# Chunks of 2048 columns in two PSUM buffers, two by two, and the first two stores as one, in an add-and-GELU kernel

## The chip, the cores and the metric

The kernel runs on one core of a Trainium2 chip. The rounds of runs were taken on several chips, each time together with the kernel before, so runs of different rounds are compared by their ratios to it. The metric is the device time in microseconds (us), median over several executions. All runs quoted are fast, with a granted clock of 1.00. The "span" of a profile is one execution as the hardware profiler saw it; it is 1.8 us below the device time of the same execution for the kernel before (120.5 for 122.32); spans compare only to within 0.3 us. A transfer "lands" when the profile has it complete.

Three compute queues and one transfer queue matter here. DVE is the vector engine, ACT the scalar (activation) engine and POOL is GpSimd; SP is the sync engine, which here only issues the transfers. The 16 transfer engines are called DMA in the profile.

## The reference

```python
x, y: float32 [1024, 4096]
z = x + y
out = 0.5 * z * (1 + tanh(sqrt(2/pi) * (z + 0.044715 * z**3)))
```

This is 33.55 MB of reads and 16.78 MB of writes for very little arithmetic. The kernel computes the same function as z * sigmoid(z * (c1 + c1 * 0.044715 * z^2)), with c1 = 2 * sqrt(2/pi).

## The kernel before

The inputs are viewed as 128 partitions of 32768 columns. x is loaded into one large buffer z, and the result is written over it. y goes through two buffers of 8192 columns in turn. The columns are worked on in chunks, each with five steps on three engines; `wt` holds the intermediate value of a chunk in PSUM.

```python
YS = 8192
CH = 1024
PS = 4                                    # PSUM buffers of one chunk
loads = [2048, 6144, 8192, 8192, 8192]    # columns, for x and for y
stores = [8192, 8192, 8192, 4096, 4096]
by_pool = set(range(1, C))                # chunk 0 is added by DVE, all others by POOL
# ... cut ...
def add(c):  # POOL:  z = z + y
def sq(c):   # ACT:   w = (root * z)^2        into PSUM
def stt(c):  # DVE:   w = (w + c1) * z
def sig(c):  # ACT:   w = sigmoid(w)
def mul(c):  # DVE:   z = w * z
# ... cut ...
for i in range(-3, C + 1):
    if 0 <= i < C:
        dve.append((stt, i))
        acts.append((sig, i))
    if 0 <= i - 1 < C:
        dve.append((mul, i - 1))
    # ... cut: the add of chunk 0 ...
    if 0 <= i + 2 < C:
        acts.append((sq, i + 2))

needs = {
    load_y: ...  # the adds that still read this y buffer
    add: ...     # the loads of these columns
    sq: lambda c: [(add, c)] + ([(mul, c - PS)] if c >= PS else []),
    store: lambda i: [(mul, c) for c in over(cr, *sr[i])],
    # ... cut ...
}
```

Every engine works through its own list strictly in order, so these lists are the schedule. In words, DVE alternates: stt of chunk i, then multiply of chunk i-1. The square of a chunk must wait until the PSUM buffer is free, that is, until the multiply of the chunk PS earlier has read it. The SP queue holds all loads, then all stores.

## Time and profile before

| | before |
|---|---|
| time, median (first 3 runs) | 122.37 us (122.04 to 122.44) |
| span of the profiled run | 120.5 us |
| DVE, ACT, POOL busy | 63%, 53%, 61% |
| transfer engines busy | 98.1% |
| moved | 50.33 MB, 418 GB/s over the span |
| last y load lands | 80.9 us |
| last store issued, landed | 104.19, 120.0 us |

Compute is over at 104 us, and the last store lands nearly 16 us later. The prediction below goes through the lines.

### The profile page before, as it was taken

The page shows a single profiled execution, that of the slowest core. Times are in us where ns is not written, and L with a number is a line of the kernel's source. Part 1 is how long each engine was busy: PE and PEld are TensorE (multiplying, and loading weights), DVE is VectorE, ACT ScalarE, POOL GpSimd, SP SyncE. Part 2 cuts the span into 40 slices and gives each one's busy share as a digit, 9 for nine tenths or more (in the row PEclk, how much of TensorE's full clock was granted, in tenths as well). Part 3 has the DMA queues.
Part 4 walks back from the last instruction along what each step waited for, and adds up shares of the span by engine and source line. Part 5 has one row for each costly group of instructions (what it writes and reads, how often), then busy time and mean ns, then how long its engine had stood idle before and what let it go on. Part 6 is the DMA issues. An engine that isn't in the chain of part 4 may idle for free.

```text
span 120.5 us, 247 instructions
## 1 busy us (share of the span) xinstructions
DVE 75.5 (63%) x66; ACT 63.8 (53%) x66; POOL 73.0 (61%) x35
## 2 busy tenths in 40 slices
DVE  0044700059999009999996999995999999500000
ACT  4016200078875048788758888883878888100000
POOL 0056000699990299999979999949999990000000
DMA  6999999989898989898989899999999999998994
GB/s 201 430 457 449 440 416 446 468 381 489 348 522 348 522 348 522 348 511 359 500 370 489 381 478 391 359 402 459 394 468 402 468 402 468 391 478 364 430 435 174
DMA packets 2162, 50.35 MB, mean 418 GB/s; under 512 B 240, under 2 KB 240, under 8 KB 240
## 3 DMA queue, kind: packets, MB, share of 16 engines
q1 hardware_dynamic: 2160, 50.33, 98.1%
q14 instruction: 2, 0.02, 0.0%
HBM read 33.55 MB, written 16.78 MB: 418 GB/s over the span
## 4 chain that ended last, share of the span: by engine, by line
DMA 49%; POOL 17%; DVE 16%; SPq 1%; ACT 1%; issue 0%; POOLq 0%
DMA y<-in_y_dram 49%; POOL z L131 17%; DVE z L151 8%; DVE w L142 8%; ACT w L136 1%; SPq L114 1%; SPq L121 0%; POOLq L131 0%
## 5 line engine op out<-in xcount | busy, mean ns | idle before, releaser
L131 POOL TENSOR_TENSOR z<-z,y 128x1024 f32<-128x1024 f32 x31 | 72.8, 2387 | 26.3 <-DMA y<-in_y_dram 26.3
L142 DVE SCALAR_TENSOR_TENSOR w<-w,z 128x1024 f32<-128x1024 f32 x32 | 39.4, 1232 | 21.3 <-ACT w L136 21.3
L136 ACT ACTIVATE w<-z 128x1024 f32<-128x1024 f32 x32 | 32.9, 1028 | 37.5 <-POOL z L131 31.6
L151 DVE TENSOR_TENSOR z<-w,z 128x1024 f32<-128x1024 f32 x32 | 38.8, 1215 | 0.0
L147 ACT ACTIVATE w<-w 128x1024 f32<-128x1024 f32 x32 | 31.4, 981 | 0.4 <-DVE w L142 0.4
L131 DVE TENSOR_TENSOR z<-z,y 128x1024 f32<-128x1024 f32 x1 | 1.2, 1226 | 6.0 <-DMA y<-in_y_dram 6.0
L190 ACT ACT_TABLE_LOAD x1 | 1.3, 1283 | 1.3 <-PEq L222 1.3
L189 DVE MEMSET one<- 128x1 f32 x1 | 0.1, 59 | 1.3 <-PEq L222 1.3
L222 POOL MEMSET const-float32-0.0<- 128x1 f32 x1 | 0.1, 98 | 0.2 <-issue 0.2
L190 ACT ACTIVATE one<-one 128x1 f32<-128x1 f32 x1 | 0.2, 203 | 0.0
L222 POOL MEMSET const-bfloat16-1.0<- 128x1 bf16 x1 | 0.1, 101 | 0.0
L222 POOL MEMSET const-uint8-127<- 128x1 uint8 x1 | 0.1, 101 | 0.0
L222 POOL MEMSET const-float32-1.0<- 128x1 f32 x1 | 0.1, 98 | 0.0
## 6 DMA issues: line engine op xcount, KB each, us to landing
z<-in_x_dram SPq DMA_DIRECT2D x3, 4096.0 KB, 34.1
y<-in_y_dram SPq DMA_DIRECT2D x3, 4096.0 KB, 24.8
out_dram<-z SPq DMA_DIRECT2D x3, 4096.0 KB, 30.6
out_dram<-z SPq DMA_DIRECT2D x2, 2048.0 KB, 17.5
z<-in_x_dram SPq DMA_DIRECT2D x1, 3072.0 KB, 13.4
y<-in_y_dram SPq DMA_DIRECT2D x1, 3072.0 KB, 20.3
z<-in_x_dram SPq DMA_DIRECT2D x1, 1024.0 KB, 4.9
y<-in_y_dram SPq DMA_DIRECT2D x1, 1024.0 KB, 6.9
```

Of the source, the lines that this page charges most:

```text
L114: nc.sync.dma_start(out=zt[:, a:b], in_=xv[:, a:b])
L131: eng.tensor_add(out=zt[:, a:b], in0=zt[:, a:b], in1=yt[s][:, o : o + b - a])
L136: nc.scalar.activation(out=wt[c], in_=zt[:, a:b], func=act.Square, scale=root)
L142: nc.vector.scalar_tensor_tensor(out=wt[c], in0=wt[c], scalar=c1, in1=zt[:, a:b], op0=alu.add, op1=alu.mult)
L147: nc.scalar.activation(out=wt[c], in_=wt[c], func=act.Sigmoid)
L151: nc.vector.tensor_mul(out=zt[:, a:b], in0=wt[c], in1=zt[:, a:b])
L189: nc.vector.memset(one, 0.0)
L190: nc.scalar.activation(out=one, in_=one, func=act.Sigmoid)
L222: nc = _bacc.Bacc("TRN2", target_bir_lowering=False, num_devices=1)
```

## The change

The intent is fewer, longer instructions: chunks of 2048 columns halve the number of instructions on three engines, so the fixed cost of each is paid half as often. Two buffers of 8 KB per partition take the same room in PSUM as the four of 4 KB before. The engines' order becomes two by two. The first two stores become one of 8 MiB, with rows of 64 KB.

```diff
-    CH = 1024
-    PS = 4
+    CH = 2048
+    PS = 2
     loads = [2048, 6144, 8192, 8192, 8192]
-    stores = [8192, 8192, 8192, 4096, 4096]
+    stores = [16384, 8192, 4096, 4096]
...
-    dve, acts = [], []
-    for i in range(-3, C + 1):
-        ... (the loop above)
+    dve = [(add, c) for c in range(C) if c not in by_pool]
+    acts = [(sq, 0), (sq, 1)]
+    for c in range(0, C, 2):
+        dve += [(stt, c), (stt, c + 1), (mul, c), (mul, c + 1)]
+        acts += [(sig, c), (sig, c + 1)]
+        if c + 2 < C:
+            acts += [(sq, c + 2), (sq, c + 3)]
```

More of the change, by code (lines that the diff above doesn't have):

```diff
@@ L158 @@
     pool = [(add, c) for c in range(C) if c in by_pool]
-    dve, acts = [], []
-    for i in range(-3, C + 1):
-        if 0 <= i < C:
-            dve.append((stt, i))
-            acts.append((sig, i))
-        if 0 <= i - 1 < C:
-            dve.append((mul, i - 1))
-        if 0 <= i + 3 < C and i + 3 not in by_pool:
-            dve.append((add, i + 3))
-        if 0 <= i + 2 < C:
-            acts.append((sq, i + 2))
+    dve = [(add, c) for c in range(C) if c not in by_pool]
[5 more added lines that the diff above has]
+            acts += [(sq, c + 2), (sq, c + 3)]
     needs = {
```

## The prediction

> **What bounds the kernel now.** I read the page first for shares, then the issues of transfers, then the time stretched over windows, then the chain of waits.
>
> The page has three compute engines at 53 to 63% of the span, and the transfer engines at 98%:
>
> ```profile
> DVE 75.5 (63%) x66; ACT 63.8 (53%) x66; POOL 73.0 (61%) x35
> ...
> DMA  6999999989898989898989899999999999998994
> ...
> q1 hardware_dynamic: 2160, 50.33, 98.1%
> HBM read 33.55 MB, written 16.78 MB: 418 GB/s over the span
> ```
>
> The row of tenths shows no slice below 8 between the first and the last two: the one queue, which carries all loads and then all stores, never runs dry. To see whether it is also at full speed I cut the span at the moments where the stores land. Columns: stretch in us, its length, busy time and count of DVE, ACT and POOL, clock, DMA share, GB/s.
>
> ```profile
> 4.00:80.90 76.90, 53.78 (x47) 45.21 (x47) 54.30 (x23) 1.00 1.01 430
> 80.90:91.10 10.20, 8.63 (x8) 7.12 (x8) 10.08 (x5) 1.00 1.01 435
> 91.10:100.70 9.60, 9.60 (x10) 8.13 (x10) 8.44 (x4) 1.00 0.99 427
> 100.70:110.40 9.70, 3.46 (x3) 1.82 (x2) 0.00 (x0) 1.00 0.98 424
> 110.40:115.30 4.90, 0.00 (x0) 0.00 (x0) 0.00 (x0) 1.00 1.01 431
> ```
>
> It holds 424 to 435 GB/s from 4 us on, and the last column does not care that compute stops at 104 us. So the bound is transfers. The ends add little: about 2 us before data flows, 1.6 us from the last bytes to the end of the span.
>
> The chain of waits could mislead. It says y loads 49%, then POOL adds, then DVE, and its last pieces are:
>
> ```profile
> 100.68 1.18 DVE w L142
> 101.86 2.30 DVE z L151 x2
> ```
>
> It stops at 104.2 us, where the last store is issued; that store lands 15.8 us later. A 2 MiB store needs 4.8 us at 435 GB/s, so most of the 15.8 us is standing in the queue behind earlier stores. That is the slack. I asked for each store's issue and its time to landing:
>
> - store 1, 4 MiB: issued 60.46, 30.6 us to landing, lands 91.1
> - store 2, 4 MiB: 66.75 + 33.9 = 100.7
> - store 3, 4 MiB: 86.84 + 23.5 = 110.3
> - store 4, 2 MiB: 96.08 + 19.1 = 115.2
> - store 5, 2 MiB: 104.19 + 15.8 = 120.0
>
> They land 9.6, 9.6, 4.9 and 4.8 us apart: 4.19 MB / 9.6 us = 437 GB/s, whatever the time of issue. The last load lands at 60.03 + 20.85 = 80.9 us and store 1 lands 10.2 us after it, so loads and stores are one unbroken train.
>
> **What the Trainium skill says.** "DMA: Bandwidth & Descriptors", section "Where 436 GB/s comes from", puts the ceiling of 16 ports at 435.2 GB/s. The trace agrees: 435 in the stretch of store 1, and 437 by landings. 50.33 MB at that ceiling are 115.7 us, of a span of 120.5.
>
> "VectorE: DVE Perf Modes", section "The TRN2 errata", gives an fp32 two-tensor operation (N+151)/0.96 ns, 2291 measured at N=2048. At N=1024 this is 1224; the trace has 1215 and 1232, so I use 2.29 us for one of 2048. Successive ones overlap: the trace's spacing is about 1.14 us for 1.22, so I use 2.21 us for the spacing.
>
> "ScalarE: Activation LUTs", section "What ACT_TABLE_LOAD costs", gives 0.833 ns per element beside a fixed part. The trace at 1024 has 1028 (square) and 981 (sigmoid); 1024 more elements add 853 ns, so 1.88 and 1.83 us.
>
> "SBUF — State Buffer", section "Who interferes with whom", says that a DVE instruction with two SBUF inputs contends with a POOL one that reads SBUF. The trace agrees: the first POOL add, beside the DVE's add at 7.4 us, took 3.39 us against a mean of 2.39.
>
> **The change, part by part.** The rows that it concerns:
>
> ```profile
> L131 POOL TENSOR_TENSOR z<-z,y 128x1024 f32<-128x1024 f32 x31 | 72.8, 2387 | 26.3 <-DMA y<-in_y_dram 26.3
> L142 DVE SCALAR_TENSOR_TENSOR w<-w,z 128x1024 f32<-128x1024 f32 x32 | 39.4, 1232 | 21.3 <-ACT w L136 21.3
> L136 ACT ACTIVATE w<-z 128x1024 f32<-128x1024 f32 x32 | 32.9, 1028 | 37.5 <-POOL z L131 31.6
> L151 DVE TENSOR_TENSOR z<-w,z 128x1024 f32<-128x1024 f32 x32 | 38.8, 1215 | 0.0
> L147 ACT ACTIVATE w<-w 128x1024 f32<-128x1024 f32 x32 | 31.4, 981 | 0.4 <-DVE w L142 0.4
> 81.02 18.52 POOL L131 TENSOR_TENSOR z<-z,y 128x1024 f32<-128x1024 f32 x8 [1.58 <-DMA y<-in_y_dram]
> ```
>
> 1. *Half as many instructions, twice as long.* DVE: 16 + 16 of 2.29 and one add of 2.29 = 33 x 2.29 = 75.6 us of records; as spacing it saves 32 x (2 x 1.14 - 2.21) = 2 us. ACT: 16 x (1.88 + 1.83) = 59 us, 4.5 us less. POOL: 15 adds; eight of 1024 took 18.52, so 4.63 us for each of 2048: 15 x 4.63 = 69 us. All of it lies beside the transfers: worth nothing in time.
>
> 2. *Chunk 0 is now the whole first load*, added by DVE alone; POOL no longer adds part of it, and the 3.39 us conflict goes. POOL's next add waits for the second y load (22.06 us) as before: nothing.
>
> 3. *The loads' releases.* The y load of the fourth piece is issued when the first y buffer has been added: 22.0 + 3 x 4.63 = 35.9 us, before 35.97. The last y load: 41.5 + 4 x 4.63 = 60.0, before 60.03. The load half stays where it is, and the last load lands at 80.9.
>
> 4. *Latency behind the last load.* With order stt, stt, mul, mul and squares that wait for multiplies two chunks earlier, a group of four chunks goes as follows from its y landing T: adds end at T+4.6, 9.3, 13.9, 18.5; second square (needs the second add) ends at 11.2; second stt 11.2 to 13.5; the first sigmoid, which ACT holds behind that square, ends at 13.0; multiplies of the first pair end at 15.7 and 17.9; third square 15.7 to 17.6, fourth 18.6 to 20.5; stt of the second pair 17.9 to 20.1 and 20.5 to 22.8; their multiplies end at 25.0 and 27.3. Before, the same group took 104.19 - 81.02 = 23.2 us. So compute ends at 81.0 + 27.3 = 108.3 us, **4.1 us later**.
>
> 5. *The stores.* The first, 8 MiB, now waits for chunk 7: 41.5 + 27.3 = 68.8 us, in place of 60.46. The queue has loads until 80.9, so 12 us are in hand. Then, at 9.65 us for 4 MiB:
>
> - store of 8 MiB: lands 80.9 + 19.5 = 100.5
> - store of 4 MiB: issued about 88.2, lands 110.2
> - 2 MiB: issued about 99.0, lands 115.0
> - 2 MiB: issued 108.3, lands 119.9
>
> Each is issued while its forerunner moves; the tightest is the last, with 115.0 - 108.3 = 6.7 us, where it had 115.2 - 104.2 = 11.0. The 4.1 us come out of slack, not out of the end.
>
> 6. *One transfer fewer, rows of 64 KB.* The packets fit 15 transfers of 128 rows (1920) and 16 small ones each (240): 2160. Now 14 x 144 = 2016. At 437 GB/s by landings nothing much is left to gain; I allow 0.2 us either way.
>
> Sum: 0 + 0 + 0 (4.1 us later, hidden) - 0.1 = a span of 120.4 and a time of about 122.3, since the profiled run was timed at 122.32 for 120.5.
>
> **Rivals.** *(a) The queue runs dry at the end.* The longer pipeline of two buffers ends late enough that the last store starts after the others are done. Against: 6.7 us in hand by step 4, in which I may be wrong by one multiply (2.3 us) or by a square (1.9), not by both and more. If compute ended at 118, the time would be 122.3 + 118 - 115 = 125.
>
> *(b) DVE becomes the bound*, as the coarse order stalls it. For: it has almost no gap in stretch 91.1 to 100.7 already (9.60 of 9.60). A group needs 8 x 2.21 = 17.7 us of DVE, plus some 9.6 us of filling, against 19.5 us between arrivals of y; the filling overlaps with the end of the group before only in part. If each group slipped by 2 us, the last would end 6 us later, at 114 us, and still be hidden; time 122.3 to 123.
>
> *(c) Long rows move differently.* A 64 KB row might be cut, or spread the 16 engines' ends apart. No view before has such a row, so this is the one thing not read off; 8 MiB at 5% less would cost 1 us. In the other direction, a saving of the gaps between packets could give 0.3 us.
>
> *(d) Gain from fewer instructions.* It speaks for faster that DVE, ACT and POOL all shed work; against, that none of them is waited for by the transfers at any time after 4 us.
>
> **Range and chances.** The three runs before spread over 0.4 us. I add 0.3 us for the rows, and a small tail upward for (a) to (c): 121.8 to 122.9. Over 2% faster would need 119.9 us, hence a span of 118.1, which needs a rate of 427 GB/s over the whole span, start and end included: 1%. Slower by 2% needs a hole of 2.5 us in the queue: 3%.
>
> **What would show each step.** Step 1: the DVE rows at 2.27 to 2.31 us x16, POOL at 4.6 to 4.7 x15. Step 3: y loads issued near 35.9 and 60.0. Step 4: the last multiply ends at 107 to 110 us. Step 5: the last store takes 11 to 13 us to land, not 15.8; DMA tenths with no new hole after slice 20; 418 GB/s over the span again. It would be wrong if a slice after 80 us falls under 8, or if the 8 MiB store lands later than about 101 us.

## The result, and the profile after

The changed kernel takes 122.25 us (121.95 to 122.35, 6 runs), the kernel before 122.25 us (122.02 to 122.50, 6 runs). The ratio is 0.9995, with a 95% interval of 0.9974 to 1.0015: the same. Ratios here are the mean time of one kernel's fast runs over that of the other's of the same rounds, so they are not quite the ratio of the medians.

The page of the changed kernel, in the parts shown of before (busy time, tenths, transfer queue):

```profile
DVE 73.7 (61%) x34; ACT 61.0 (51%) x34; POOL 67.5 (56%) x19
...
DMA  6999999989898989898999999998899889898994
...
q1 hardware_dynamic: 2016, 50.33, 98.3%
HBM read 33.55 MB, written 16.78 MB: 419 GB/s over the span
```

All three engines have less to do, and the transfers are as full as before, with no slice below 8 between the first and the last two. The groups of instructions on the same page:

```profile
L131 POOL TENSOR_TENSOR z<-z,y 128x2048 f32<-128x2048 f32 x15 | 67.3, 4518 | 31.3 <-DMA y<-in_y_dram 31.3
L142 DVE SCALAR_TENSOR_TENSOR w<-w,z 128x2048 f32<-128x2048 f32 x16 | 36.7, 2296 | 26.5 <-ACT w L136 26.2
L136 ACT ACTIVATE w<-z 128x2048 f32<-128x2048 f32 x16 | 30.1, 1882 | 38.5 <-POOL z L131 29.4
L151 DVE TENSOR_TENSOR z<-w,z 128x2048 f32<-128x2048 f32 x16 | 35.8, 2281 | 0.0
L147 ACT ACTIVATE w<-w 128x2048 f32<-128x2048 f32 x16 | 29.7, 1855 | 4.4 <-DVE w L142 4.4
```

Each instruction takes nearly twice what it took, and there are half as many. The idle time is in the last columns. That of POOL grew about as much as its busy time fell: it waits 31.3 us for y, where it waited 26.3. The waits of DVE and ACT grew by some 5 us too, more than their busy time fell (1.8 and 2.8 us), because their work also ends later. Time taken out of an engine that was not awaited has become waiting on that engine.

What the change really moved is seen in the timeline of the last group: the adds, the later instructions of DVE and the last squares of ACT. Columns: start, length, engine, line, operation, tiles, count, and in brackets the idle time before it and what ended it. First the end of the kernel before (its adds are in the prediction, 81.02 + 18.52 = 99.54 us), then the changed kernel:

```profile
99.57 1.03 ACT L136 ACTIVATE w<-z 128x1024 f32<-128x1024 f32 x1 [0.36 <-POOL z L131]
...
100.63 1.23 DVE L142 SCALAR_TENSOR_TENSOR w<-w,z 128x1024 f32<-128x1024 f32 x1
101.77 2.39 DVE L151 TENSOR_TENSOR z<-w,z 128x1024 f32<-128x1024 f32 x2
```

```profile
81.05 17.96 POOL L131 TENSOR_TENSOR z<-z,y 128x2048 f32<-128x2048 f32 x4 [2.07 <-DMA y<-in_y_dram]
...
94.21 4.48 DVE L151 TENSOR_TENSOR z<-w,z 128x2048 f32<-128x2048 f32 x2
...
96.58 1.88 ACT L136 ACTIVATE w<-z 128x2048 f32<-128x2048 f32 x1 [0.39 <-DVE z L151]
98.61 4.65 DVE L142 SCALAR_TENSOR_TENSOR w<-w,z 128x2048 f32<-128x2048 f32 x2
99.04 1.88 ACT L136 ACTIVATE w<-z 128x2048 f32<-128x2048 f32 x1 [0.58 <-POOL z L131]
...
103.16 4.48 DVE L151 TENSOR_TENSOR z<-w,z 128x2048 f32<-128x2048 f32 x2
```

The last group of y lands at the same time as before (POOL starts at 81.05, before 81.02), but the last multiply ends at 103.16 + 4.48 = 107.6 us, 3.5 us later than before. The stores absorb it. The record of the last store, before and after:

```profile
L125 SPq DMA_DIRECT2D out_dram<-z x1: 332/332/332, 104.2 to 104.2; - x1
DMA to landing us min/median/max: 15.8/15.8/15.8
...
L125 SPq DMA_DIRECT2D out_dram<-z x1: 332/332/332, 107.7 to 107.7; - x1
DMA to landing us min/median/max: 12.0/12.0/12.0
```

Issue and landing of each store, read in the same way:

| columns | before: issued, to landing, lands | after: issued, to landing, lands |
|---|---|---|
| first 8192 | 60.46 + 30.6 = 91.1 | |
| up to 16384 | 66.75 + 33.9 = 100.7 | 68.21 + 32.1 = 100.3 |
| up to 24576 | 86.84 + 23.5 = 110.3 | 87.64 + 22.3 = 109.9 |
| up to 28672 | 96.08 + 19.1 = 115.2 | 98.72 + 16.1 = 114.8 |
| up to 32768 | 104.19 + 15.8 = 120.0 | 107.67 + 12.0 = 119.7 |

In every row that both have, the changed kernel issues the store later and it lands at the same time within 0.4 us. The last one is issued 3.5 us later and needs 3.8 us less to land. That is what slack looks like in such a view: a later start with a shorter stay in the queue.

### The profile page after: what moved, and what is told of

Read it like the earlier page. It is cut to its first block, busy times and chain, and to the rows that moved or that the text cites. A ratio compares the mean times of both kernels' runs of the same rounds, so it can differ in the third digit from the quotient of the medians.

```text
span 120.2 us, 174 instructions
## 1 busy us (share of the span) xinstructions
DVE 73.7 (61%) x34; ACT 61.0 (51%) x34; POOL 67.5 (56%) x19
## 2 busy tenths in 40 slices
DMA packets 2017, 50.33 MB, mean 419 GB/s; under 512 B 225, under 2 KB 225, under 8 KB 225
## 3 DMA queue, kind: packets, MB, share of 16 engines
q1 hardware_dynamic: 2016, 50.33, 98.3%
## 4 chain that ended last, share of the span: by engine, by line
DMA 50%; POOL 26%; POOLq 4%; DVE 4%; DVEq 2%; ACT 2%; SPq 1%; issue 0%
DMA y<-in_y_dram 50%; POOL z L131 26%; POOLq L201 4%; DVE w L142 2%; DVEq L201 2%; DVE z L151 2%; ACT w L136 2%; SPq L114 1%; SPq L121 1%; POOLq L131 0%
## 5 line engine op out<-in xcount | busy, mean ns | idle before, releaser
L131 POOL TENSOR_TENSOR z<-z,y 128x2048 f32<-128x2048 f32 x15 | 67.3, 4518 | 31.3 <-DMA y<-in_y_dram 31.3
L142 DVE SCALAR_TENSOR_TENSOR w<-w,z 128x2048 f32<-128x2048 f32 x16 | 36.7, 2296 | 26.5 <-ACT w L136 26.2
L136 ACT ACTIVATE w<-z 128x2048 f32<-128x2048 f32 x16 | 30.1, 1882 | 38.5 <-POOL z L131 29.4
L151 DVE TENSOR_TENSOR z<-w,z 128x2048 f32<-128x2048 f32 x16 | 35.8, 2281 | 0.0
L147 ACT ACTIVATE w<-w 128x2048 f32<-128x2048 f32 x16 | 29.7, 1855 | 4.4 <-DVE w L142 4.4
L131 DVE TENSOR_TENSOR z<-z,y 128x2048 f32<-128x2048 f32 x1 | 2.3, 2292 | 6.1 <-DMA y<-in_y_dram 6.1
## 6 DMA issues: line engine op xcount, KB each, us to landing
out_dram<-z SPq DMA_DIRECT2D x1, 4096.0 KB, 22.3
```

Of the source, the lines that this page charges most:

```text
L131: eng.tensor_add(out=zt[:, a:b], in0=zt[:, a:b], in1=yt[s][:, o : o + b - a])
L136: nc.scalar.activation(out=wt[c], in_=zt[:, a:b], func=act.Square, scale=root)
L142: nc.vector.scalar_tensor_tensor(out=wt[c], in0=wt[c], scalar=c1, in1=zt[:, a:b], op0=alu.add, op1=alu.mult)
L147: nc.scalar.activation(out=wt[c], in_=wt[c], func=act.Sigmoid)
L151: nc.vector.tensor_mul(out=zt[:, a:b], in0=wt[c], in1=zt[:, a:b])
```

## The experiments

The theory is that the one queue of transfers sets the time, that nothing in the change touches its bytes or its rate, and that the 3.5 us by which compute is later come out of slack. The rivals are that two effects of the change cancel; that 64 KB rows move at another rate; that compute sets the end after all; and that compute is hidden however late it is. Twelve kernels were run. None of them asks what sets the rate of the transfers, some 437 GB/s between landings: the one queue, the 16 engines or the memory. That stays open.

### Each half of the change alone

`chunks_only` is the changed kernel with the five stores of before; `stores_only` is the kernel before with the merged store.

```diff
 chunks_only:  -    stores = [16384, 8192, 4096, 4096]
               +    stores = [8192, 8192, 8192, 4096, 4096]
 stores_only:  the reverse edit, in the kernel before
```

> The changed kernel with the five stores of before. Theory (transfers bound, 4.1 us of compute hidden): 122.3 us, within 0.3 of before; last multiply at 107.7 us as in the changed kernel, last store 12 us to landing. Rival (the two parts of the change cancel: coarse chunks cost about what the merged store gains): 122.8 or more here, and stores_only faster by the same amount.

> The kernel before with the first two stores as one. Theory: 122.3 us, within 0.3 of before; the 8 MiB store is issued at 66.7 us, lands near 100.5. Rival (the parts cancel): 121.8 or less. Rival (64 KB rows move slower): the 8 MiB store lands after 101.5 us and the time is over 122.8.

Measured: `chunks_only` 122.32 us, ratio to before 1.0009 (0.9989 to 1.0028). `stores_only` 122.20 us, ratio 1.0000 (0.9978 to 1.0021). Nothing cancels: each half is worth nothing to within 0.3%. The later end of compute belongs to the chunks: their last store is issued at 107.62 us and takes 12.1 us, as in the changed kernel, while `stores_only` has 104.16 and 15.9, as before. In `stores_only` the 8 MiB store is issued at 66.79 us and lands at 100.8, the second store of before at 100.7. So rows of 64 KB move at the rate of rows of 32 KB.

One reading of this pair is a warning. In windows, the stretch from 80.7 to 100.3 us of `stores_only` reads so (columns as in the prediction):

```profile
4.00:80.70 76.70, 53.54 (x47) 44.96 (x47) 54.32 (x23) 1.00 1.03 438
80.70:100.30 19.60, 18.09 (x16) 15.12 (x16) 18.51 (x8) 1.00 0.93 402
```

Taken alone, 402 GB/s would speak for slower long rows, and the 438 ahead of it for faster loads. The landings contradict both. The share of 1.03 ahead of it, above what 16 engines have, shows that packets are not counted exactly where their bytes move. With packets of 64 KB, rates over such stretches are too rough to decide 5%; times of landing, and the total time, are not.

### The transfers without any compute

```diff
-    pool = [(add, c) ...]; dve = ...; acts = ...
+    pool, dve, acts = [], [], []
     needs: load_y, store  ->  []      # wrong result on purpose; only loads precede stores
```

> All loads and stores of the changed kernel, no add, square, stt, sigmoid or multiply (wrong result on purpose). Theory: the loads and stores alone take what the kernel takes, 121.8 to 122.4 us. Rival (compute sets the end, or slows the transfers by using the same memory): clearly less, 118 us or below. A further use: if all waits are gone and it is still 122, no order of the compute can win more than the difference.

Measured: 121.89 us, ratio to before 0.9982 (0.9957 to 1.0007). The page confirms that nothing else runs:

```profile
DVE 0.1 (0%) x1; ACT 1.5 (1%) x2; POOL 0.2 (0%) x4
...
q1 hardware_dynamic: 2016, 50.33, 98.1%
```

The loads and stores alone take what both kernels take: 0.2% less than the kernel before, and 0.4% (0.5 us) less at the most by the interval. So with these transfers in this queue no order of the compute can gain more than that, nor does compute slow the transfers by more.

### One load fewer, in both kernels

The last y load of 4 MiB is left out; the last 8192 columns use the y of the piece before, so the result is wrong.

```diff
-        sp += [(load_x, i), (load_y, i)]
+        sp += [(load_x, i)] + ([(load_y, i)] if i < 4 else [])
 ...
     def add(c):
         s, o = divmod(a, YS)
+        s = min(s, 2)
```

> The kernel before without the last y load of 4 MiB (the last 8192 columns take the y of the piece before: wrong result on purpose). Theory: 9.65 us less in the queue and compute still ends before the queue needs it (estimated last multiply at 102 us, needed by 105): 112.6 us, give or take 0.5. Rival (the chain of adds and multiplies sets the end): only as much as compute ends earlier, 2 us: 120.

> The changed kernel without the last y load (wrong result on purpose), to be set against the kernel before with the same cut. Theory: the queue is 9.65 us shorter, but compute ends only 2 us earlier (estimated 105.6 us), so the slack that the long chunks used up is gone: the last store is issued after the one in front has moved, a hole of 1 to 3 us, 113.5 to 115 us, 1 to 2.5 us over the kernel before with the same cut. Rival (long chunks cost nothing at all anywhere): the same 112.6 us.

Measured: the kernel before becomes 112.55 us, ratio 0.9214, that is 9.6 us less. 4.19 MB at 435 GB/s are 9.64 us. The time follows the bytes one for one, and the rival, that the chain of adds and multiplies sets the end, would have given 120. The changed kernel becomes 114.28 us, ratio 0.9327. The two ratios were taken in different sets of rounds; by the spans of the profiled runs, 110.7 against 112.2, the changed kernel is 1.5 us longer (1.4 by the ratios, 1.7 by the times as they stand). Its tenths show where (the kernel before without the load has no such hole: its last store goes out at 102.69 us and still stands in the queue, 7.5 us to landing):

```profile
DMA  6999999998998998999899899888899489888295
```

The 2 near the end is the hole. The last store is issued at 105.38 us and lands in 6.3 us, with nothing ahead of it: the store in front had landed at 96.4 + 7.8 = 104.2. The 4 further ahead costs nothing: there the 8 MiB store gives way to the next one, and these two land at 89.7 and 99.4, 9.7 us apart as elsewhere. This is the cost of the long chunks that the full kernel hides: with 10 us fewer in the queue, the slack is gone and some 1.5 us of the delay show.

### Delaying the last store

Idle multiplies on a scratch tile are put ahead of the last multiply.

```diff
     def mul(c):
+        if c == C - 1:
+            for _ in range(k):            # k = 2 or 4
+                nc.vector.tensor_mul(out=late, in0=late, in1=late)   # 128x2048
```

> The changed kernel with two idle multiplies of 128x2048 on the vector engine just ahead of the last multiply: the last store is issued 4.5 us later, at 112.2 us. Theory (some 6 us in hand at the end): 122.2 to 122.7 us. Rival (the end of compute sets the time): 126.8.

> As after_late2 with four idle multiplies: the last store is issued 8.9 us later, at 116.6 us. Theory: the queue has run dry at about 114, and the store needs 4.8 us and some 2 us to start and to be confirmed: 125 to 127 us. Rival (compute is hidden however late): 122.3.

> The kernel before with the same four idle multiplies ahead of its last one: the last store is issued at 113.1 us. Theory (3.5 us more in hand than in the changed kernel): 122.3 to 123.5 us, 2.5 to 3.5 us less than the changed kernel with the same delay. Rival (both kernels have the same slack): as late as after_late4.

| kernel | last store issued | to landing | time | ratio to before |
|---|---|---|---|---|
| changed | 107.67 | 12.0 | 122.25 | 0.9995 |
| changed, k = 2 | 112.1 | 7.5 | 122.27 | 0.9984 (0.9960 to 1.0008) |
| changed, k = 4 | 117.0 | 6.3 | 125.84 | 1.0276 (1.0255 to 1.0296) |
| before, k = 4 | 113.4 | 6.8 | 122.31 | 0.9986 (0.9964 to 1.0008) |

This measures the slack directly. A store of 2 MiB on an empty queue takes 6.3 us from issue to landing. For a landing at 120.0 it must be issued by 113.7. The kernel before issues at 104.2 and had 9.5 us in hand; the changed kernel issues at 107.7 and has 6.0 (5.7 if its own landing at 119.7 is the mark). A delay within that is free (4.4 us, and 9.2 us in the kernel before); the delay to 117.0 is 3.3 to 3.6 us past the edge and costs 2.76% of 122.5, 3.4 us. Both rivals fall: compute does not set the end, nor is it hidden without limit. The windows of the changed kernel with k = 4 show the empty queue itself:

```profile
113.00:116.00 3.00, 3.00 (x2) 0.00 (x0) 0.00 (x0) 1.00 0.35 147
116.00:117.00 1.00, 0.97 (x1) 0.00 (x0) 0.00 (x0) 1.00 0.00 0
117.00:118.00 1.00, 0.00 (x0) 0.00 (x0) 0.00 (x0) 1.00 0.61 262
```

Between 116 and 117 us DVE is busy (0.97, the last multiply) and not one byte moves.

### Merging stores one step further

```diff
-    stores = [16384, 8192, 4096, 4096]
+    stores = [16384, 16384]
```

> The changed kernel with two stores of 8 MiB, the merging carried one step further. Theory: the second waits for the last multiply at 107.7 us while the first lands at 100.3, so the queue stands empty for about 8 us: second lands near 107.7 + 19.3 + 2 = 129, time about 131 us. Rival (fewer and longer transfers are good in themselves): 122 or less.

Measured: 130.99 us, ratio 1.0720. The second store waits for the last multiply, goes out at 107.27 us and takes 20.8 us, to 128.1. The first had landed at 68.09 + 31.8 = 99.9. So merging is free only while the merged store is still issued before the queue has emptied. The first two stores may be merged because loads fill the queue until 80.9 us; the last ones may not.

### Order, length and number of buffers

Where do the 3.5 us of delay come from? `long_one_by_one` is the changed kernel with the order of before, `short_two_by_two` the kernel before with the order of the change.

> The changed kernel (2048 columns, two buffers, merged store) with the one-by-one order of before: stt of the next chunk, then multiply of this one. Theory: time 122.3 whatever the order; the last store's issue tells what of the 3.5 us delay is order: if the length of the chunks alone makes it, 107 to 108 us; if the order does, nearer 105.

> The kernel before (1024 columns, four buffers, five stores) with the order stt, stt, mul, mul. Theory: time 122.3; last store issued at 104 to 106 us. If the order makes the delay of 3.5 us, 107 or later.

Measured: `short_two_by_two` 122.51 us (2 runs, ratio 1.0025), last store issued at 104.36. The order alone delays compute by 0.2 us, no more than this moment differs between runs with the same compute (107.27 us in `stores_two`, 107.67 in the changed kernel). But `long_one_by_one` took 135.05 us, ratio 1.1052, where the theory expected 122.3. This is a plain miss. Its timeline in the second group:

```profile
46.12 1.88 ACT L136 ACTIVATE w<-z 128x2048 f32<-128x2048 f32 x1 [2.84 <-POOL z L131]
47.94 1.83 ACT L147 ACTIVATE w<-w 128x2048 f32<-128x2048 f32 x1
48.03 2.30 DVE L142 SCALAR_TENSOR_TENSOR w<-w,z 128x2048 f32<-128x2048 f32 x1 [2.00 <-ACT w L136]
50.24 2.28 DVE L151 TENSOR_TENSOR z<-w,z 128x2048 f32<-128x2048 f32 x1
52.61 1.88 ACT L136 ACTIVATE w<-z 128x2048 f32<-128x2048 f32 x1 [2.84 <-DVE z L151]
```

In brackets is what ended the idle time before the instruction. The square at 52.61 waits for the multiply that ended at 52.5, because that multiply frees the buffer that the square writes, while the other buffer still holds the chunk in between; the next stt waits for that square (2.00 us, as at 48.03). Square, stt and multiply follow one another with no overlap: 52.61 - 46.12 = 6.49 us for each chunk, where POOL delivers one each 4.48. Compute falls behind, and the last store goes out at about 126 us.

If that is right, two buffers with short chunks must do the same. The last run tests it: the kernel before with `PS = 2` and nothing else.

> The kernel before (1024 columns, one-by-one order, five stores) with two PSUM buffers in place of four; it follows the miss of long_one_by_one, 135 us where 122.3 was expected. New theory: with two buffers and the one-by-one order each square waits for the multiply that has just ended and the next stt waits for that square, so a chunk takes stt 1.14 + multiply 1.22 + square 1.03 + waits 0.15 = 3.5 us where POOL gives one each 2.31: the last store is issued near 128 us, time 134 to 139 us. Rival (the 2048 columns made long_one_by_one slow): 122.3.

Measured: 139.53 us, ratio 1.1398. Its timeline has the same waits:

```profile
48.84 1.03 ACT L136 ACTIVATE w<-z 128x1024 f32<-128x1024 f32 x1 [1.56 <-DVE z L151]
...
49.91 1.23 DVE L142 SCALAR_TENSOR_TENSOR w<-w,z 128x1024 f32<-128x1024 f32 x1 [1.15 <-ACT w L136]
51.05 1.22 DVE L151 TENSOR_TENSOR z<-w,z 128x1024 f32<-128x1024 f32 x1
52.36 1.03 ACT L136 ACTIVATE w<-z 128x1024 f32<-128x1024 f32 x1 [1.57 <-DVE z L151]
```

A chunk takes 3.51 us (squares at 45.34, 48.84, 52.36), as expected; the last store is issued at 131.0 us, 3 us later than expected, and the time is 0.5 us above the range that was given. So the length of the chunks is not to blame: two buffers in the one-by-one order are.

This shows what the two-by-two order in the change is for. With stt, stt, mul, mul, one more multiply lies between the multiply that frees a buffer and the stt that needs the square, and the square (1.88 us) fits under it (2.28 us). Within the change the order is no matter of taste: it takes the place of the two buffers that were given up. As for the 3.5 us, two by two costs at most 0.2 us with short chunks and four buffers, and the rest comes with the long chunks and two buffers. No run separates these two, but the two timelines of the last group, shown above, do. The last square of the changed kernel starts at 99.04, as soon as the last add has ended (99.01), so no buffer holds it up; the one before it does wait for a buffer, but it ends at 98.46, before DVE is free for its stt at 98.61. What grew is the tail behind the last add, a square, an stt and two multiplies in both kernels: from 104.16 - 99.54 = 4.6 us to 107.64 - 99.01 = 8.6 us. These 4.0 us, less the 0.5 us by which the adds end sooner, are the 3.5. So it is the length of the chunks; the two buffers cost nothing there.

## Why the prediction was right

**The bound.** It rested on the queue's tenths, its rate in stretches and the even landings of the stores. After the change the tenths and the landings held; the rates in stretches read 401 to 438 GB/s, which the landings correct, as told under `stores_only`. Beyond that, `transfers_only` gave the same time without compute, and one load fewer took off its transfer time.

**Step 1, the sizes.** 2.29 us for each DVE instruction (measured 2.296 and 2.281) and 1.88 for the square (1.882) were right, and so was 1.83 for the sigmoid within 0.03 (1.855). POOL came out at 4.48 us of spacing, not 4.63: doubling the short add's spacing was too cautious, since a fixed part of 0.15 us is saved. The sum for DVE was right: its records add up to 75.5 us (75.6 predicted), and without their overlaps DVE is busy 1.8 us less than before (2 predicted). The sum for POOL was 1.5 us too high, and for ACT 2 us too low, mostly because it left out the table load of 1.3 us; none of it mattered.

**Step 3, the loads.** Predicted issues of y at 35.9 and 60.0 us; measured 35.67 and 59.57, landing of the last at 80.9 as predicted.

**Step 4, the latency.** Predicted 4.1 us later, at 108.3 us; measured 3.5 us, at 107.6. Most of the difference is the POOL term: the fourth add ends at 99.0 us, where 81.0 + 18.5 = 99.5 was predicted. The time alone would not have tested this step: even 9.2 us of delay left the kernel before at 122.31 us (`before_late4`). What confirms the step is the timeline.

**Step 5, the slack.** Predicted landings of 100.5, 110.2, 115.0 and 119.9 us; measured 100.3, 109.9, 114.8 and 119.7. The slack itself was mis-sized a little. The prediction measured it to the landing of the store in front (6.7 us left of 11.0). The delay runs put it at 6.0 of 9.5, because the store in front has moved its last bytes before it lands, and a store must be issued some time before its own first byte moves: in `after_late4` the store in front lands at 115.0 us but nothing moves after 114.5, and the last store, issued at 116.99, moves nothing until 117.75. So the right yardstick is the landing wanted less the 6.3 us of a store on an empty queue. By the same term the sum of rival (a), 122.3 + issue - 115, is too low: for the issue at 117.0 it gives 124.3 us, and 125.84 was measured.

**Step 6, the rows.** 2016 packets, as counted, and no effect on the rate.

**The sum.** The time of 122.3 us is met more closely than its parts: the span was 120.2 us and not 120.4, and the time lies 2.1 us above it and not 1.8. That these two differences cancel is luck, of 0.2 to 0.3 us. In the range, the rate for a gain of 2% should read 426 GB/s (50.33 MB in 118.1 us), not 427; and the 6.7 us under rival (a) come from step 5, not from step 4.

**The rivals.** A dry queue at the end did not occur, and appears only with another 6 us of delay or a shorter queue. DVE did not become the bound. The prediction had the waits for the two buffers in step 4, in the order of the changed kernel. It did not ask what another order would cost, and the miss of `long_one_by_one`, an expectation written later, shows how much hangs on it: with the order of before the same chunks are 10.5% slower.

## What to carry to other kernels

When transfers fill the span, ask of each change only whether a transfer is issued later than the queue needs it; compare the time from issue to landing with what the same transfer takes on an empty queue, and the difference is the slack that a change may spend. Merge transfers only where the queue is still full when the merged one becomes ready. When buffers are halved to make tiles longer, check in the engines' orders how many instructions lie between the one that frees a buffer and the one that needs its next contents: here one multiply between them was the difference between 122 and 135 us.

## What the Trainium skill lacked or had wrong

- "SBUF — State Buffer", section "Summary: rules for kernel authors", advises some 358 GB/s for transfers between HBM and SBUF. A core that runs alone moved 419 GB/s over the whole span and 4.19 MB each 9.6 us (437 GB/s) between landings; by the advice the 50.33 MB would need an estimated 140.6 us. "HBM Reference", section "Specifications (TRN2)", says that a core alone measures well above its share, and this is what the runs show.
- "DMA: Bandwidth & Descriptors", section "Anatomy of one DMA", fits 2.0 us + bytes / 436 GB/s for transfers issued from GpSimd. For a 2 MiB store issued from SP on an empty queue the fit, which is none for SP, gives an estimate of 6.8 us; four runs here show 6.3 (the last store of `less_y_after`, `after_late4`, `long_one_by_one`'s third store and `short_two_buffers`' last).
- No page says whether rows of 64 KB move differently from rows of 32 KB in a store: they did not (0.9978 to 1.0021).
- "Perfetto Trace Analysis", section "Identifying Performance Opportunities", says that bubbles that repeat can mean too few buffers, which agrees with `long_one_by_one`. No page adds that the order of the instructions decides how many are enough: with chunks of 2048 columns two buffers took 135.05 us in the one-by-one order and 122.25 us two by two.
- No page warns that rates read over a stretch from packet records mislead with packets of 64 KB: from 80.7 to 100.3 us of the changed kernel they give 401 GB/s, where its 8 MiB (8.39 MB) between the landings at 80.9 and 100.3 us make 432.
